# Adding three partial products into the same 256 PSUM columns, in the input and up-projections of a hybrid RWKV-7 / latent-attention layer

## The chip, the cores and the metric

The kernel runs on one core of a Trainium2 chip. The metric is device time in microseconds (us) of one execution, the median of several runs. TensorE (PE in the profile) does the matmuls and loads weights (PEld), VectorE is DVE, ScalarE is ACT, GpSimd is POOL, and SyncE (SP) issues most DMAs.

## The reference

One decoder layer over 256 tokens of width 2048, in float32:

```python
h = rms_norm(x, attn_norm_g[l])
proj = h @ w_in[l]
shifted = token_shift(proj[..., :RWKV_SHIFT_DIM], rwkv_mu[l])
h_r, h_k, h_v, h_w, h_a, h_g = _split(shifted, IN_SPLITS[:6])
c_q, c_kv, k_pe = _split(proj[..., RWKV_SHIFT_DIM:], IN_SPLITS[6:])
y_rwkv = rwkv7_mixer(h_r, h_k, h_v, h_w, h_a, h_g, ...)
y_mla = mla_mixer(c_q, c_kv, k_pe, positions, ...)
x = x + concatenate([y_rwkv, y_mla]) @ w_out[l]
h = rms_norm(x, ffn_norm_g[l])
x = x + conv_glu_ffn(h, ...)
return rms_norm(x, final_norm_g)
```

`rwkv7_mixer` is a recurrence over 16 heads of 64, with a group norm and a gate behind it. `mla_mixer` is causal attention with 8 heads; it normalises `c_q` and `c_kv` (512 wide each) and projects them up to queries (`w_uq`), keys and values. `conv_glu_ffn` is a gated MLP of width 5632. The input projection has 3360 + 1024 + 64 columns, the up-projections of queries and keys 20 tiles of 128 columns.

## The kernel before, in words

A float32 product is made from three products of shorter numbers. Weights and activations are each split into a high part (the value rounded to the type that PE reads fast, fp32r) and a low part (what is left). The kernel adds w_hi·x_hi + w_hi·x_lo + w_lo·x_hi.

Weights come in pieces of 128 x 1024 (`piece`, L125 to L137): SP loads `raw`, ACT casts it to `hi` (L133), DVE subtracts to get `lo` (L134; for the second piece of input tiles 17 to 24 POOL does). The high and low parts of the activations lie side by side, as 2 x 256 columns for each step of 128 rows.

`prod_b` multiplies one piece: for each step a 512-wide matmul of w_hi against [x_hi | x_lo] (L165), so that columns 0:256 of the PSUM tile hold w_hi·x_hi and columns 256:512 hold w_hi·x_lo; then for each step a 256-wide matmul of w_lo against x_hi, into columns 0:256 (L168). `joined` evicts the tile in three operations: ACT copies columns 256:512 (L173), DVE adds columns 0:256 (L174), DVE multiplies by a scale for each token (L175). The scale is that of the RMS norm: `rsB` for the input, `rrB` for the two latents.

`in_tile(i)` (L191) makes one of 35 output tiles of 128 columns of the input projection, from two pieces of 8 steps, 32 matmuls in all. `up_b` (L797) makes two up tiles of 4 steps each from one piece; there are 20 up tiles: 4 `qr` (rotary queries), 8 `qn` and 8 `kn`. The FFN uses `prod_b` and `joined` too (L961 to L972).

`shifted` (L371) evicts an input tile into `h` and mixes it with its neighbour token; that feeds the recurrence's preparation. Gram products of the prepared rows (`gram`, PE L527, evicted at L532 into `G`) go to DRAM by DMA (`dL`, L540) and back in another layout (`Lp`, L569). DVE scales `Lp` (L578) and solves triangular systems in 31 steps (L582, L584). While that runs, PE goes on with input tiles 18 and up. Then follow the latent tiles `cr`, the up-projections of the rotary queries and the values, the chunks of the recurrence (L677, with `px`, `pS`, `py` in PSUM and `XB`, `UV`, `ST` made by DVE), the other up-projections, the group norm (L719 to L741: `gmu`, `gva`, `gsq`, with a reciprocal square root `ry` on POOL), transposes `pyT` (L745) for the output product, the attention scores (`psc`, `mx`, `pexp`), the output projection and the FFN.

A PSUM tile comes from one of three rings: `mm` with 3 tiles, `ch` with 3, `at` with 2. Rings of SBUF hold 3 `raw`, 3 `hi`, 3 `lo` and 7 small tiles. The order of instructions in each engine's queue isn't that of the code: a scheduler that simulates the timeline sets it, by operands, rings and its own costs, on all engines (SP's only in the opening is written by hand). So a change of an eviction can move other instructions.

Of the kernel before, what the change touches and what calls it, by code (L numbers as in the profile page):

```python
# [14 lines left out]
ALU = mybir.AluOpType  # L15
AX = mybir.AxisListType

P = 128
T = 256
# [35 lines left out]
def hybrid_layer(ctx: ExitStack, tc: tile.TileContext, a: dict, out: bass.AP):  # L55
    nc = tc.nc
    V, S, PE = nc.vector, nc.scalar, nc.tensor
# [8 lines left out]
    def nm(s):  # L66
        uid[0] += 1
        return f"{s}{uid[0]}"
# [3 lines left out]
    def s4(dt=F32, n="s4"):  # L72
        return sb.tile([P, 1024], dt, tag="s4", name=nm(n), bufs=NS4)
# [11 lines left out]
    def t1(n, w=T, dt=F32):  # L85
        return sb.tile([P, 260], dt, tag="t1", name=nm(n), bufs=NT1)[:, :w]

    def t2(n, w=T, dt=F32):
        return sb.tile([P, 384], dt, tag="t2", name=nm(n), bufs=NT2)[:, :w]

    def st(n, w):
        return sb.tile([P, 32], F32, tag="st", name=nm(n), bufs=8)[:, :w]

    def mm(n="mm"):
        return ps.tile([P, 512], F32, tag="mm", name=nm(n), bufs=NMM)
# [4 lines left out]
    def at(n="at"):  # L100
        return ps.tile([P, 512], F32, tag="at", name=nm(n), bufs=NAT)

    def con(shape, n, dt=F32):
        return sb.tile(shape, dt, name=n, bufs=1)
# [10 lines left out]
    def vv(name, i, rows=slice(0, P)):  # L115
        return vec[rows, VOFF[name] + i:VOFF[name] + i + 1]
# [8 lines left out]
    def piece(src, dst=None, eng=None):  # L125
        raw = sb.tile([P, 1024], F32, tag="raw", name=nm("raw"), bufs=NRAW)
        last_w[0] = nc.sync.dma_start(raw, src).ins
        if dst is None:
            hi = sb.tile([P, 1024], F32R, tag="hi", name=nm("hi"), bufs=NHI)
            lo = sb.tile([P, 1024], F32R, tag="lo", name=nm("lo"), bufs=NLO)  # L130
        else:
            hi, lo = (dst.rearrange("p k t -> p (k t)")[:, q * 1024:(q + 1) * 1024] for q in range(2))
        S.copy(hi, raw)  # L133
        sub = (eng or V).tensor_tensor(lo, raw, hi.bitcast(F32), ALU.subtract).ins  # L134
        if eng is None:
            last_lo[0] = sub
        return hi, lo  # L137

    def xsplit(g):
        raw = s4(n="xraw").rearrange("p (k t) -> p k t", k=4)  # L140
        nc.sync.dma_start(raw, xT[:, g * 4:(g + 1) * 4, :])
        for j in range(4):
            k = g * 4 + j
            h = xs_[g][:, j, 0, :]
            S.activation(h, raw[:, j, :], AF.Copy, scale=vv("ag", k))
            last_x[0] = V.scalar_tensor_tensor(xs_[g][:, j, 1, :], raw[:, j, :], vv("ag", k),
                                               h.bitcast(F32), ALU.mult, ALU.subtract).ins
        return raw
# [5 lines left out]
    def flush(every=False):  # L154
        now = [f for n, f in pend if n == 0 or every]
        pend[:] = [(n - 1, f) for n, f in pend if n > 0 and not every]
        for f in now:
            f()
# [3 lines left out]
    def prod_b(acc, pieces, act, kt0, n, first, last):  # L162
        hi, lo = pieces
        for j in range(n):
            PE.matmul(acc, hi[:, j * P:(j + 1) * P], act(kt0 + j), start=first and j == 0, stop=False,  # L165
                      skip_group_check=True)
        for j in range(n):
            PE.matmul(acc[:, :T], lo[:, j * P:(j + 1) * P], act(kt0 + j)[:, 0, :], start=False,  # L168
                      stop=last and j == n - 1, skip_group_check=True)


    def joined(dst, acc, scale, rows=slice(0, P)):
        S.copy(dst, acc[rows, T:])  # L173
        V.tensor_tensor(dst, acc[rows, :T], dst, ALU.add)  # L174
        V.tensor_tensor(dst, dst, scale[rows], ALU.mult)  # L175


    def prod_a(accs, pieces, act_hi, act_lo, kt0, n, first, last, tbs=(0, 1)):
# [10 lines left out]
    x_hl = lambda k: xs_[k // 4][:, k % 4, :, :]  # L189

    def in_tile(i, pf=mm):  # L191
        acc = pf()
        for h in range(2):
            eng = nc.gpsimd if h and 17 <= i < 25 else None
            prod_b(acc, piece(a["win"][i, h], eng=eng), x_hl, h * 8, 8, h == 0, h == 1)
        flush()
        return acc

# [108 lines left out]
    acc0 = [mm(), mm(), at()]  # L307
    pcs = {}
# [4 lines left out]
    def sums(h):  # L313
        for tb in range(2):
            t, o = s4(n="xt"), h * 2 + tb
            nc.sync.dma_start(t, a["x"][tb * P:(tb + 1) * P, h * 1024:(h + 1) * 1024])
            S.activation(t, t, AF.Square, accum_out=ssx[:, o:o + 1])

    with tc.manual_schedule(engines={mybir.EngineType.SP}):
        for g in range(4):  # L320
            xsplit(g)
            if g == 0:
                nc.scalar.dma_start(cst, a["cst"])
            if g % 2 == 0:
                for i in range(2):
                    pcs[i, g // 2] = piece(a["win"][wt0[i], g // 2])
            for i in range(2):
                hl = tuple(u[:, (g % 2) * 512:(g % 2 + 1) * 512] for u in pcs[i, g // 2])
                prod_b(acc0[i], hl, x_hl, g * 4, 4, g == 0, g == 3)
        for h in range(2):  # L330
            prod_b(acc0[2], piece(a["win"][26, h]), x_hl, h * 8, 8, h == 0, h == 1)
        sums(0)
        kacc[0] = in_tile(1)
        dve0 = last_lo[0]
        sums(1)
        kacc[1] = in_tile(2, ch)
        rope_tables()
        lora = s4(n="lora")
        nc.sync.dma_start(lora, a["lora"])

    rsB = sb.tile([P, T], F32, tag="rsB", name="rsB", bufs=1)
# [30 lines left out]
    def shifted(acc, i, rows=slice(0, P), dst=None):  # L372
        h = t1("h", 257)
        nc.gpsimd.memset(h[rows, 0:1], 0.0)
        joined(h[rows, 1:257], acc, rsB, rows)
        o = t1("sh") if dst is None else dst
        S.activation(o[rows], h[rows, 1:257], AF.Copy, scale=om_mu[rows, i:i + 1])
        V.scalar_tensor_tensor(o[rows], h[rows, 0:256], vv("mu", i, rows), o[rows], ALU.mult, ALU.add)
        return o
# [49 lines left out]

    acc = acc0[2]  # L430
    kraw, ksw = t1("kraw"), t1("ksw")
    joined(kraw[0:64], acc, rsB, slice(0, 64))
    shifted(acc, 26, rows=slice(64, 96), dst=sg2)
    sigmoid_(sg2, slice(64, 96))
    nc.gpsimd.dma_start(kraw[64:128], kraw[0:64])
# [11 lines left out]
    for p in range(8):  # L447
        pp, g = p // 2, p % 2
# [3 lines left out]
        acc = kacc[p] if p in kacc else in_tile(1 + p)  # L452
# [45 lines left out]
    for p in range(8):  # L498
        pp, g = p // 2, p % 2
        acc = in_tile(9 + p)  # L500
# [254 lines left out]
    cl, rrs, rrB = [], [], []  # L755

    def latent(x, gname, post):
        c_ = [s4(F32R, "cl").rearrange("p (k s t) -> p k s t", k=2, s=2) for _ in range(2)]
        ssum = t2("css")
        for j in range(4):  # L760
            acc = in_tile(27 + x * 4 + j)
            cr = t2("cr")
            joined(cr, acc, rsB)
            if j == 0:
                S.activation(ssum, cr, AF.Square)
            else:
                sq = t2("csq")
                S.activation(sq, cr, AF.Square)
                V.tensor_tensor(ssum, ssum, sq, ALU.add)
            h_, l_ = (c_[j // 2][:, j % 2, q, :] for q in range(2))  # L770
            S.activation(h_, cr, AF.Copy, scale=vv(gname, j))
            V.scalar_tensor_tensor(l_, cr, vv(gname, j), h_.bitcast(F32), ALU.mult, ALU.subtract)
        pss = at("pss")
        for tb in range(2):
            PE.matmul(pss[:, tb * 2:tb * 2 + 2], ssum[:, tb * P:(tb + 1) * P], ones[:, 0:2], start=True, stop=True)
        m = st("ssm", 2)
        V.tensor_copy(m, pss[:, 0:4:2])
        rr = con([P, 2], f"rr{x}")
        V.tensor_scalar(rr, rsqrt(m, 1.0 / 512, EPS, 2), post, None, ALU.mult)
        rb = con([P, T], f"rrB{x}")  # L780
        bcast(rr, rb, at, t2)
        rrs.append(rr)
        rrB.append(rb)
        cl.append(c_)
# [12 lines left out]
    def up_b(src, i, x, dsts):  # L797
        pcs = piece(src[i])
        for j in range(2):
            acc = mm()  # L800
            prod_b(acc, (pcs[0][:, j * 512:(j + 1) * 512], pcs[1][:, j * 512:(j + 1) * 512]),
                   lambda k: cl[x][k // 2][:, k % 2, :, :], 0, 4, True, True)
            joined(dsts[j], acc, rrB[x])

    for i in range(4, 6):
        up_b(a["wuq"], i, 0, [qr[:, (i - 4) * 2 + j, :] for j in range(2)])
# [145 lines left out]
    for blk, nf in enumerate((24, 20)):  # L952
        hh = [s4(F32R, "hh").rearrange("p (k t) -> p k t", k=4) for _ in range(nf // 4)]
        hl = [s4(F32R, "hl").rearrange("p (k t) -> p k t", k=4) for _ in range(nf // 4)]
        for fi in range(nf):
            f = f0 + fi
            accs = []
            for gu in range(2):
                acc = mm()
# [24 lines left out]
        n = nf // 2  # L984
# [105 lines left out]
```

## Time and profile before

| | us |
|---|---|
| median of 3 runs | 1208.74 (1208.29 to 1209.25) |
| span of the profiled execution | 1203.6 |
| PE busy | 1159.9 (96% of the span) |
| DVE busy | 839.1 (70%) |
| ACT busy | 599.4 (50%) |
| POOL busy | 77.4 (6%) |

The profiled execution's own time is its span, 1203.6 us; what lies around the span makes up the rest of the 1208.74. Rows of the trace give the start and the length in us, engine, line of the kernel, operation, output and inputs by name, shape and how many instructions; in square brackets the engine's idle time before it and what ended that. Rows of groups give the smallest, median and largest duration in ns. The rows of the table by stage begin with the stretch and its length, then the busy time of each engine with the number of instructions, the granted clock of PE, the share of time in which DMA engines worked, and GB/s.

### The profile page before, as it was taken

How to read it: one execution, taken by the hardware profiler on the slowest of the kernel's cores; microseconds unless marked ns; L12 is line 12 of the kernel's file. 1: busy time of each engine (PE TensorE's matmuls, PEld its weight loads, DVE VectorE, ACT ScalarE, POOL GpSimd, SP SyncE). 2: the span in 40 equal slices, each digit the busy share in tenths (PEclk: the TensorE clock that was granted, in tenths of full speed). 3: DMA queues.
4: the chain of work that ended last, by engine and by line, in shares of the span. 5: the costliest groups of instructions: out<-in, count | busy, mean ns of one | idle time of the engine just before them, and what ended most of it. 6: DMA issues, size and time to landing. Idle time of an engine off the chain costs nothing.

```text
span 1203.6 us, 18439 instructions
## 1 busy us (share of the span) xinstructions
PE 1159.9 (96%) x6993; PEld 990.6 (82%) x6993; DVE 839.1 (70%) x1352; ACT 599.4 (50%) x939; POOL 77.4 (6%) x214
## 2 busy tenths in 40 slices
PE   7899998998799999999999999999999999999996
PEld 6788877887577888888888888888888888888885
DVE  6898749977887556777777776444577777775563
ACT  6784434633444455655555554333455555554442
POOL 1500042002110001000000000000000000000000
PEclk9899998999999999999999999999999999999999
DMA  8555443754133555655555555555655555566662
GB/s 317 177 155 159 138 143 122 213 168 147 62 140 114 184 172 175 206 190 191 187 192 191 191 192 191 193 190 190 200 191 192 192 193 193 192 223 202 205 217 81
DMA packets 71017, 215.82 MB, mean 179 GB/s; under 512 B 17616, under 2 KB 17872, under 8 KB 70928
## 3 DMA queue, kind: packets, MB, share of 16 engines
q1 hardware_dynamic: 69776, 211.84, 53.9%
q10 hardware_dynamic: 768, 2.05, 0.5%
q8 instruction: 55, 0.90, 0.3%
q0 software_dynamic: 384, 0.75, 0.2%
q14 instruction: 34, 0.28, 0.1%
HBM read 210.48 MB, written 3.41 MB: 178 GB/s over the span
## 4 chain that ended last, share of the span: by engine, by line
PE 84%; DVE 8%; DMA 3%; POOL 2%; issue 1%; ACT 1%; SPq 1%; ACTq 0%; DVEq 0%; POOLq 0%
PE mm L165 34%; PE mm L168 17%; PE mm L185 9%; PE mm L187 9%; PE mm L186 9%; DVE lo L134 2%; PE pg L527 1%; DMA xt<-in_x 1%; PE px L677 1%; DMA Lp<-dL 1%; DMA raw<-in_win 0%; POOL cosR L291 0%; DMA dT<-Tq 0%; PE py L677 0%; SPq L540 0%
## 5 line engine op out<-in xcount | busy, mean ns | idle before, releaser
L134 DVE TENSOR_TENSOR lo<-raw,hi 128x1024 fp32r<-128x1024 f32 x368 | 453.0, 1231 | 288.0 <-ACT hi L133 283.1
L133 ACT CAST hi<-raw 128x1024 fp32r<-128x1024 f32 x376 | 395.5, 1052 | 451.7 <-issue 234.9
L165 PE MATMUL mm<-z,hi 128*128 128x512 f32 x1408 | 351.3, 392 | 0.0
L165 PEld LDWEIGHTS mm<-z,hi 128*128 128x128 f32 x1408 | 251.9, 188 | 43.7
L168 PEld LDWEIGHTS mm<-z,lo 128*128 128x128 f32 x1408 | 188.3, 188 | 14.5
L168 PE MATMUL mm<-z,lo 128*128 128x256 f32 x1408 | 191.6, 278 | 0.0
L165 PE MATMUL mm<-x,hi 128*128 128x512 f32 x528 | 144.4, 410 | 17.9 <-DVE h L174 9.6
L186 PE MATMUL mm<-lo,hh 128*128 128x512 f32 x336 | 130.7, 389 | 0.0
L187 PE MATMUL mm<-hi,hl 128*128 128x512 f32 x336 | 130.7, 389 | 0.0
L165 PEld LDWEIGHTS mm<-x,hi 128*128 128x128 f32 x528 | 97.0, 195 | 35.6 <-ACT hi L133 8.3
L185 PE MATMUL mm<-hi,hh 128*128 128x512 f32 x336 | 119.7, 389 | 0.0
L168 PEld LDWEIGHTS mm<-x,lo 128*128 128x128 f32 x528 | 74.7, 193 | 7.4 <-issue 1.0
L168 PE MATMUL mm<-x,lo 128*128 128x256 f32 x528 | 79.9, 288 | 0.0
L186 PEld LDWEIGHTS mm<-lo,hh 128*128 128x128 f32 x336 | 63.1, 188 | 13.1
L187 PEld LDWEIGHTS mm<-hi,hl 128*128 128x128 f32 x336 | 63.1, 188 | 13.1
L185 PEld LDWEIGHTS mm<-hi,hh 128*128 128x128 f32 x336 | 63.1, 188 | 13.0
L186 PE MATMUL mm<-lo,yhi 128*128 128x512 f32 x128 | 51.1, 399 | 0.0
L187 PE MATMUL mm<-hi,ylo 128*128 128x512 f32 x128 | 50.5, 394 | 0.0
L185 PE MATMUL mm<-hi,yhi 128*128 128x512 f32 x128 | 49.6, 405 | 0.0
L964 POOL MEMSET gt<- 128x2 f32 x44 | 4.3, 100 | 575.8 <-DVE hl L976 558.9
L187 PEld LDWEIGHTS mm<-hi,ylo 128*128 128x128 f32 x128 | 24.1, 188 | 5.6 <-DVE ylo L749 0.4
L185 PEld LDWEIGHTS mm<-hi,yhi 128*128 128x128 f32 x128 | 23.9, 188 | 5.7 <-DVE kn L174 0.8
(291 smaller groups left out, 1142.8 us busy)
## 6 DMA issues: line engine op xcount, KB each, us to landing
raw<-in_wgu SPq DMA_DIRECT2D x176, 512.0 KB, 3.3
raw<-in_wdn SPq DMA_DIRECT2D x88, 512.0 KB, 4.1
raw<-in_win SPq DMA_DIRECT2D x70, 512.0 KB, 3.7
raw<-in_wout SPq DMA_DIRECT2D x32, 512.0 KB, 3.4
raw<-in_wuq SPq DMA_DIRECT2D x6, 512.0 KB, 3.3
xraw<-in_xT SPq DMA_DIRECT2D x4, 512.0 KB, 6.3
xt<-in_x SPq DMA_DIRECT2D x4, 512.0 KB, 6.7
raw<-in_wuv SPq DMA_DIRECT2D x4, 512.0 KB, 3.3
```

What stands on the lines that cost most here:

```text
L133: S.copy(hi, raw)
L134: sub = (eng or V).tensor_tensor(lo, raw, hi.bitcast(F32), ALU.subtract).ins
L165: PE.matmul(acc, hi[:, j * P:(j + 1) * P], act(kt0 + j), start=first and j == 0, stop=False, skip_group_check=True)
L168: PE.matmul(acc[:, :T], lo[:, j * P:(j + 1) * P], act(kt0 + j)[:, 0, :], start=False, stop=last and j == n - 1, skip_group_check=True)
L185: PE.matmul(accs[tb], ah, wh, start=first and j == 0, stop=False)
L186: PE.matmul(accs[tb], ah, wl, start=False, stop=False)
L187: PE.matmul(accs[tb], al, wh, start=False, stop=last and j == n - 1)
L527: PE.matmul(pg[h][:, o:o + P], BK[pp][hs, gg, w * 2 + r, :, :], AR[pp][hs, gg, w * 2 + r, :, :], start=o == 0, stop=True, skip_group_check ...
L677: PE.matmul(dst[HS[h], a_ * 64:(a_ + 1) * 64], lhsT, rhs, start=n == 0 and a_ == 0, stop=True, skip_group_check=True)
L964: nc.gpsimd.memset(gt[:, 0:2], 0.0)
```

## The change

A new product `prod_c` splits each 512-wide matmul in two of 256, w_hi·x_hi and w_hi·x_lo, and adds both, and the w_lo·x_hi product, into columns 0:256. Columns 256:512 stay unused. A new eviction `scaled` is one DVE operation: columns 0:256 times the scale. The input tiles (`in_tile` and the three of the opening) and the up tiles use the two; the FFN keeps `prod_b` and `joined`. Lines of the new kernel behind the new functions lie 12 further down.

```diff
--- before.py
+++ after.py
@@ -168,11 +168,23 @@
             PE.matmul(acc[:, :T], lo[:, j * P:(j + 1) * P], act(kt0 + j)[:, 0, :], start=False,
                       stop=last and j == n - 1, skip_group_check=True)
 
-
-    def joined(dst, acc, scale, rows=slice(0, P)):
-        S.copy(dst, acc[rows, T:])
-        V.tensor_tensor(dst, acc[rows, :T], dst, ALU.add)
-        V.tensor_tensor(dst, dst, scale[rows], ALU.mult)
+    def prod_c(acc, pieces, act, kt0, n, first, last):
+        hi, lo = pieces
+        for j in range(n):
+            for s in range(2):
+                PE.matmul(acc[:, :T], hi[:, j * P:(j + 1) * P], act(kt0 + j)[:, s, :],
+                          start=first and j == 0 and s == 0, stop=False)
+        for j in range(n):
+            PE.matmul(acc[:, :T], lo[:, j * P:(j + 1) * P], act(kt0 + j)[:, 0, :], start=False,
+                      stop=last and j == n - 1)
+
+    def joined(dst, acc, scale):
+        S.copy(dst, acc[:, T:])
+        V.tensor_tensor(dst, acc[:, :T], dst, ALU.add)
+        V.tensor_tensor(dst, dst, scale, ALU.mult)
+
+    def scaled(dst, acc, scale, rows=slice(0, P)):
+        V.tensor_tensor(dst, acc[rows, :T], scale[rows], ALU.mult)
 
 
     def prod_a(accs, pieces, act_hi, act_lo, kt0, n, first, last, tbs=(0, 1)):
@@ -192,7 +204,7 @@
         acc = pf()
         for h in range(2):
             eng = nc.gpsimd if h and 17 <= i < 25 else None
-            prod_b(acc, piece(a["win"][i, h], eng=eng), x_hl, h * 8, 8, h == 0, h == 1)
+            prod_c(acc, piece(a["win"][i, h], eng=eng), x_hl, h * 8, 8, h == 0, h == 1)
         flush()
         return acc
 
@@ -326,9 +338,9 @@
                     pcs[i, g // 2] = piece(a["win"][wt0[i], g // 2])
             for i in range(2):
                 hl = tuple(u[:, (g % 2) * 512:(g % 2 + 1) * 512] for u in pcs[i, g // 2])
-                prod_b(acc0[i], hl, x_hl, g * 4, 4, g == 0, g == 3)
+                prod_c(acc0[i], hl, x_hl, g * 4, 4, g == 0, g == 3)
         for h in range(2):
-            prod_b(acc0[2], piece(a["win"][26, h]), x_hl, h * 8, 8, h == 0, h == 1)
+            prod_c(acc0[2], piece(a["win"][26, h]), x_hl, h * 8, 8, h == 0, h == 1)
         sums(0)
         kacc[0] = in_tile(1)
         dve0 = last_lo[0]
@@ -372,7 +384,7 @@
     def shifted(acc, i, rows=slice(0, P), dst=None):
         h = t1("h", 257)
         nc.gpsimd.memset(h[rows, 0:1], 0.0)
-        joined(h[rows, 1:257], acc, rsB, rows)
+        scaled(h[rows, 1:257], acc, rsB, rows)
         o = t1("sh") if dst is None else dst
         S.activation(o[rows], h[rows, 1:257], AF.Copy, scale=om_mu[rows, i:i + 1])
         V.scalar_tensor_tensor(o[rows], h[rows, 0:256], vv("mu", i, rows), o[rows], ALU.mult, ALU.add)
@@ -429,7 +441,7 @@
 
     acc = acc0[2]
     kraw, ksw = t1("kraw"), t1("ksw")
-    joined(kraw[0:64], acc, rsB, slice(0, 64))
+    scaled(kraw[0:64], acc, rsB, slice(0, 64))
     shifted(acc, 26, rows=slice(64, 96), dst=sg2)
     sigmoid_(sg2, slice(64, 96))
     nc.gpsimd.dma_start(kraw[64:128], kraw[0:64])
@@ -760,7 +772,7 @@
         for j in range(4):
             acc = in_tile(27 + x * 4 + j)
             cr = t2("cr")
-            joined(cr, acc, rsB)
+            scaled(cr, acc, rsB)
             if j == 0:
                 S.activation(ssum, cr, AF.Square)
             else:
@@ -798,9 +810,9 @@
         pcs = piece(src[i])
         for j in range(2):
             acc = mm()
-            prod_b(acc, (pcs[0][:, j * 512:(j + 1) * 512], pcs[1][:, j * 512:(j + 1) * 512]),
+            prod_c(acc, (pcs[0][:, j * 512:(j + 1) * 512], pcs[1][:, j * 512:(j + 1) * 512]),
                    lambda k: cl[x][k // 2][:, k % 2, :, :], 0, 4, True, True)
-            joined(dsts[j], acc, rrB[x])
+            scaled(dsts[j], acc, rrB[x])
 
     for i in range(4, 6):
         up_b(a["wuq"], i, 0, [qr[:, (i - 4) * 2 + j, :] for j in range(2)])
```

## The prediction

> **What bounds the kernel now.** I read the sums by stage first: busy time of PE, PEld (its weight loads), DVE, ACT and POOL, the granted PE clock, DMA share and GB/s.
>
> ```profile
> 60.00:177.00 117.00, 116.55 (x739) 100.32 (x739) 91.88 (x186) 61.59 (x105) 17.32 (x26) 1.00 0.47 142
> 177.00:188.00 11.00, 4.99 (x19) 4.02 (x18) 6.95 (x20) 2.95 (x7) 0.82 (x4) 0.70 0.56 211
> 188.00:242.00 54.00, 52.44 (x311) 45.73 (x309) 51.20 (x98) 32.00 (x55) 7.77 (x7) 1.00 0.59 171
> 242.00:288.00 46.00, 45.53 (x673) 39.55 (x672) 35.40 (x70) 19.88 (x35) 8.83 (x32) 1.00 0.49 150
> 288.00:326.00 38.00, 26.31 (x465) 22.48 (x464) 29.58 (x45) 11.92 (x23) 5.13 (x14) 0.96 0.23 82
> 326.00:369.00 43.00, 40.82 (x203) 30.20 (x201) 37.56 (x76) 18.83 (x44) 6.14 (x14) 1.00 0.38 133
> 480.00:1203.00 723.00, 713.91 (x3813) 615.77 (x3811) 473.77 (x658) 352.84 (x499) 4.11 (x41) 1.00 0.58 191
> ```
>
> From 480 us on, PE works 713.91 of 723 us: that is the FFN, which the change leaves alone. What can be gained lies before. There PE waits at 177 to 188 (4.99 of 11 us busy) and from 288 to 326 (26.31 of 38); DVE is at 95% (51.20 of 54) in 188:242, yet PE at 97% too, so not much is lost there. The second view is the chain that ended last, in the FFN, where the same product runs undisturbed (start, length, what), and the sum of L165 over a long piece of it.
>
> ```profile
> 482.94 1.83 PE mm L165 x8
> 484.77 0.91 PE mm L168 x8
> 485.68 1.83 PE mm L165 x8
> 487.51 0.94 PE mm L168 x8
> ```
>
> ```profile
> 482.93:731.03 248.10, 179.44 (x721) 128.71 (x721) 1.00 0.57 192
> ```
>
> Eight 512-wide matmuls take 1.83 us (229 ns each), eight 256-wide ones 0.91 to 0.94. The 721 matmuls in 248.10 us are 90 such groups, so a whole group of 8 + 8 takes 248.10/90 = 2.757 us, and 2.757 − 1.83 = 0.927 is 8 × 116 ns. The third view is the chain around the wait at 177.8, and the engines' own rows there.
>
> ```profile
> 166.18 1.98 PE pg L527 x24
> ...
> 174.15 1.55 DMA dL<-G
> ...
> 175.82 6.07 DMA Lp<-dL
> ...
> 181.92 1.24 DVE Lp L578
> ...
> 183.66 0.34 DVE h L174
> ...
> 184.05 3.78 PE mm L165 x8
> ```
>
> ```profile
> 176.98 1.07 PE L168 MATMUL mm<-x,lo 128*128 128x256 f32 x8
> 184.05 3.78 PE L165 MATMUL mm<-x,hi 128*128 128x512 f32 x8 [6.01 <-DVE h L174]
> 187.63 1.37 PE L168 MATMUL mm<-x,lo 128*128 128x256 f32 x8
> ```
>
> ```profile
> 179.60 1.23 DVE L134 TENSOR_TENSOR lo<-raw,hi 128x1024 fp32r<-128x1024 f32 x1 [6.43 <-ACT hi L133]
> ```
>
> The last Gram product ends at 168.16. Its result goes to DRAM (dL) and back (Lp, 6.07 us), and DVE scales it at 181.92. In DVE's queue the eviction of input tile 18 stands behind that scaling, so tile 21, which needs that PSUM buffer, waits 6.01 us. The clock then falls: its first 8 matmuls take 3.78 us instead of 1.83, the next 1.37 instead of 1.07. The stall costs 6.0 + 1.95 + 0.3 = 8.3 us.
>
> **The change part by part.**
>
> *Split of the 512-wide matmul.* 35 input tiles with 16 and 20 up tiles with 4 make 640 hi matmuls; each becomes two of 256. Eight pairs take 16 × 0.116 = 1.853 us against 1.83, that is +0.023, and 80 such groups give **+1.9 us**. With 0.91 or 0.94 per eight it is −0.8 to +4. The added weight loads are the point to check. Their rows in the FFN (min, median, max in ns) are these:
>
> ```profile
> L168 PEld LDWEIGHTS mm<-z,lo x1408: 187/188/188, 469.2 to 1084.6; 128*128 128x128 f32 x176
> ```
>
> A load lasts 188 ns, yet the 256-wide matmuls, each with a load of its own, follow each other every 116 ns and add into the same columns: the loads overlap, and same-column accumulation costs nothing extra. PE waits for neither.
>
> The Trainium skill speaks against this ("TensorE: Matmul & The Clock Gate", Part 3, The mechanism: a weight load overlaps running matmuls only if its row group differs). By that rule the sum would be the last rival's below; this trace's 116 ns disagrees.
>
> *Evictions.* What goes are the copy L173 (ACT), the sum L174 and one of two DVE operations; one stays. The sums up to 470 us of L173, L174 and L175:
>
> ```profile
> 0.00:470.00 470.00, 20.28 (x56) 0.98 0.51 162
> ```
> ```profile
> 0.00:470.00 470.00, 23.31 (x56) 0.98 0.51 162
> ```
> ```profile
> 0.00:470.00 470.00, 23.29 (x56) 0.98 0.51 162
> ```
>
> With 55 or 56 evictions by 0.37 and 0.42 us, 20 us of ACT and 23 us of DVE go. Where PE is over 97% busy they are hidden, so they are counted by stage only.
>
> *177 us.* PE, around the last Gram (pg); mm_1921 is input tile 19, before:
>
> ```order
> L165 MATMUL mm_1921<-x_66,hi_1924 128x512 x4
> L168 MATMUL mm_1921<-x_65,lo_1925 128x256 x4
> L527 MATMUL pg_1709<-AR_498,BK_502 128x128 x4
> L527 MATMUL pg_1722<-AR_498,BK_502 128x128 x2
> L527 MATMUL pg_1723<-AR_498,BK_502 128x128 x2
> ```
>
> and after, where mm_2054 is input tile 18:
>
> ```order
> L178 MATMUL mm_2054<-x_65,lo_2058 128x256
> L539 MATMUL pg_2002<-AR_574,BK_578 128x128 x4
> L178 MATMUL mm_2054<-x_65,lo_2058 128x256 x2
> L539 MATMUL pg_2003<-AR_574,BK_578 128x128 x4
> L559 MATMUL pt_2032<-cst,BK_578 128x128 x2
> L178 MATMUL mm_2054<-x_65,lo_2058 128x256
> L178 MATMUL mm_2054<-x_66,lo_2058 128x256 x4
> ```
>
> So the last Gram moves one input tile ahead. DVE at the eviction of tile 18 (h_1904 before, h_2198 after), first before:
>
> ```order
> L134 TENSOR_TENSOR lo_2040<-raw_2037,hi_2039 128x1024
> L134 TENSOR_TENSOR lo_2093<-raw_2090,hi_2092 128x1024
> L578 TENSOR_TENSOR Lp_1766<-Lp_1766,Mp 128x1024
> L582 TENSOR_TENSOR tm_1822<-Tq_1821,Lp_1766 128x31
> L584 TENSOR_TENSOR Tq_1821<-Tq_1821,tm_1822 128x31
> L174 TENSOR_TENSOR h_1904<-mm_1776,h_1904 128x256
> ```
>
> and after:
>
> ```order
> L134 TENSOR_TENSOR lo_2284<-raw_2281,hi_2283 128x1024
> L590 TENSOR_TENSOR Lp_2046<-Lp_2046,Mp 128x1024
> L134 TENSOR_TENSOR lo_2360<-raw_2357,hi_2359 128x1024
> L594 TENSOR_TENSOR tm_2116<-Tq_2115,Lp_2046 128x31
> L187 TENSOR_TENSOR h_2198<-mm_2054,rsB 128x256
> L596 TENSOR_TENSOR Tq_2115<-Tq_2115,tm_2116 128x31
> L187 TENSOR_TENSOR h_2274<-mm_2213,rsB 128x256
> ```
>
> The eviction still stands behind the Lp scaling, now with a lo behind it, and all DVE work queued there waits for the load Lp. Before, from the Gram's end to the scaling went 181.92 − 168.16 = 13.76 us; scaling, lo, one small operation and the eviction add 1.24 + 1.23 + 0.2 + 0.42, so tile 21 can start some 16.8 us behind the Gram. PE has meanwhile the rest of tile 18 (about 4.3 us of Gram, transposes and lo products) and two tiles of 5.5 us (2 × 2.757): 15.3 us, against 177.8 − 168.2 = 9.7 before. A wait of 1.5 us is left of 6.0, too short, I think, to bring the clock down. −4.5 − 1.95 − 0.3 = −6.8; I take **−6**, since SP's queue has other transfers there. Bounds: −8.3 (all of it) and 0 (the Gram's inputs come no earlier on DVE, and PE waits for them instead).
>
> *Start, and 60:242.* At 42 us PE waits for an eviction:
>
> ```profile
> 42.59 3.75 PE L165 MATMUL mm<-x,hi 128*128 128x512 f32 x8 [3.20 <-DVE h L174]
> ```
> ```profile
> 40.55 0.42 DVE L229 COPY rsB<-rsb 128x256 f32<-128x256 f32 x1
> ```
>
> The sum at 42.02 did not need the norm scale rsB; the new single operation does. But rsB is copied at 40.55, ahead of it in the same queue before and after: nothing lost, nothing won here, −0.5 for the later 8 us (bounds −3 to 0). In 188:242 PE is idle 1.56 us (54 − 52.44): −0.5 (0 to −1.6).
>
> *288 to 369.* The reachable waits are these, on PE:
>
> ```profile
> 321.59 0.74 PE L168 MATMUL mm<-cl,lo 128*128 128x256 f32 x4 [2.13 <-DVE lo L134]
> ...
> 323.18 1.02 PE L677 MATMUL py<-UV,G 128*64 128x64 f32 x15 [0.85 <-DVE UV L694]
> ```
> ```profile
> 369.13 1.17 PE L745 MATMUL pyT<-cst,yt 128*128 128x128 f32 x8 [1.97 <-DVE yt L741]
> ```
>
> The recurrence's own waits on XB and UV hold no eviction, since the q evictions begin only at 324.6:
>
> ```profile
> L174 DVE TENSOR_TENSOR qn<-mm,qn x8: 406/418/425, 324.6 to 352.4; 128x256 f32<-128x256 f32 x8
> ```
>
> After the change the scores' maxima (mx) and the second group norm (gmu) come behind the last up-projection on DVE, before:
>
> ```order
> L849 TENSOR_REDUCE mx_3805<-psc_3803 128x1
> L719 TENSOR_REDUCE gmu_3846<-yt_2408 128x16
> L174 TENSOR_TENSOR kn_3346<-mm_3666,kn_3346 128x256
> ```
>
> and after:
>
> ```order
> L187 TENSOR_TENSOR kn_3834<-mm_4264,rrB_3822 128x256
> L134 TENSOR_TENSOR lo_4552<-raw_4549,hi_4551 128x1024
> L861 TENSOR_REDUCE mx_4333<-psc_4331 128x1
> L861 TENSOR_REDUCE mx_4349<-psc_4347 128x1
> L861 TENSOR_REDUCE mx_4333<-psc_4331 128x1
> L731 TENSOR_REDUCE gmu_4374<-yt_2784 128x16
> ```
>
> DVE's chain from gmu to the transposes pyT ran from here to 369.13:
>
> ```profile
> 344.39 1.21 DVE L719 TENSOR_REDUCE gmu<-yt 128x16 f32<-128x1024 f32 x1
> ...
> 361.33 1.23 DVE L727 TENSOR_TENSOR yt<-yt,ry 128x1024 f32<-128x1024 f32 x1 [1.94 <-POOL ry L219]
> ```
>
> 24.7 us, 5.7 of it evictions and lo that are gone from it; what stands ahead of gmu adds 2.7: 21.7 us from the last up-projection. PE has meanwhile 18 output products, the rest of two score sets, four gates and four score sets, from these rows about 18.5 us (4.1 for four gate matmuls, 1.73 per score set):
>
> ```profile
> 355.07 1.02 PE L739 MATMUL pgate<-g2a,sg 128*128 128x512 f32 x2
> ...
> 359.18 0.50 PE L185 MATMUL mm<-hi,yhi 128*128 128x512 f32 x1
> ...
> 363.81 0.32 PE L838 MATMUL psc<-cmb,idb 128*128 128x384 bf16 x1 [0.26 <-ACT pexp L850]
> ...
> 365.54 0.32 PE L838 MATMUL psc<-cmb,idb 128*128 128x384 bf16 x1
> ```
>
> The pyT wait becomes 3.2 instead of 1.97, +1.2 (up to +4.2 if no DVE work leaves the chain). Ahead of it the waits of 2.13 and 0.85 go, because the up tiles fill in: −3. Net **−2**; bounds −6.4 (these waits, the pyT wait and shorter DVE turns) and +4.2.
>
> Sum: +1.9 − 6 − 0.5 − 0.5 − 2 = −7.1. The span was 1203.6, the median of the runs 1208.74, 5.1 more for what lies around it; I leave that as it is. 1208.7 − 7.1 = **1201.6 us**.
>
> **The rivals.**
>
> *No change.* The freed time was hidden, and Lp comes as late as before because the Gram's inputs are made by the same DVE chain (91.88 of 117 us busy in 60:177, so there is slack that hides evictions). Only the split is left: 1208.7 + 1.9 = 1210.6, or 1208 with small gains. Against it: the Gram stands earlier in PE's queue, and some 20 evictions before it have each lost one of 0.42, 8 us of DVE work.
>
> *Slower.* The group norm's chain, moved behind the last up-projection, decides: pyT waits 6.2 instead of 1.97 (+4.2), with +1.9 for the split, and the gain at 177 fails: 1214.8. It turns the sign as soon as 177 gives back less than about 6 us. For it: DVE is the late one at 369. Against: with the evictions gone, DVE reaches gmu earlier.
>
> *Bare weight loads.* If each added load of 188 ns were exposed, 640 × 0.188 = 120 us: 1329. The steady 116 ns rows are against it. This is the rule on row groups in the Trainium skill ("TensorE: Matmul & The Clock Gate", Part 3, The mechanism) taken as it is written.
>
> **How the numbers follow.** Forecast 0.65, no change 0.14, slower rival 0.18, bare loads 0.03. The measurement can tell about 0.2%, 2.4 us. The forecast's own ends, all at once, are −20.1 and +8.2; they won't all meet. I go from 1190, where the wait at 177 and most of the waits after 288 are gone, to 1213, which holds no change and half of the slower case. Left out: bare loads, the worst of the slower case, some of the best. Chances: faster 0.65, same 0.14, slower 0.21.
>
> **What would show it.** In the profile after: eight hi pairs on the chain of input tiles in 1.83 to 1.88 us; up to 470 us no row of the copy or the sum (L173, L174 before) and one DVE row of 0.42 us per eviction; PE's wait before tile 21 at 1 to 3 us and a clock of 1.00 there; the wait before pyT at 3 us. Wrong: pairs of eight over 2 us, a wait on pg's inputs (AR, BK) of 4 us or more ahead of the Gram, a wait of 6 us at tile 21, or one over 5 us at pyT. The FFN should take as long as before.

## The result, and the profile after

| | before | changed |
|---|---|---|
| median of 6 runs each, us | 1209.14 (1208.29 to 1212.53) | 1200.43 (1196.53 to 1201.20) |
| ratio to before, 95% interval | | 0.992 (0.9896 to 0.9944) |
| span of the profiled execution, us | 1203.6 | 1198.3 |
| PE busy / idle in the span, us | 1159.9 / 43.7 | 1164.2 / 34.1 |
| DVE, ACT busy, us | 839.1, 599.4 | 817.5, 582.9 |

The kernel is faster by 0.8%, 8.7 us between the medians. The two profiled executions differ by 5.3 us only: that of before was one of its faster ones (its span with the 1.7 us that lay around the changed kernel's, 1200.04 against 1198.3, makes 1205.3). In every run on record whose span is known, 1.7 to 1.9 us lie around the span; so most of the 5.1 us that were put down to it ahead of the result (1208.74 − 1203.6) is the difference between runs. What follows splits the 5.3 us: PE idles 9.6 us less and works 4.3 us more.

The table by stage of the changed kernel (stretch, its length, busy time of PE, PEld, DVE, ACT, POOL, granted PE clock, DMA share, GB/s):

```profile
60.00:177.00 117.00, 117.00 (x999) 113.81 (x998) 81.24 (x167) 56.66 (x87) 16.96 (x28) 1.00 0.49 150
177.00:188.00 11.00, 8.51 (x72) 8.25 (x71) 10.66 (x23) 6.69 (x13) 3.67 (x4) 1.00 0.41 137
188.00:242.00 54.00, 50.94 (x569) 50.29 (x567) 47.19 (x85) 24.31 (x36) 6.88 (x9) 0.97 0.66 196
288.00:326.00 38.00, 36.08 (x454) 29.00 (x453) 32.45 (x47) 15.13 (x24) 5.97 (x14) 1.00 0.42 140
326.00:369.00 43.00, 38.77 (x230) 32.71 (x230) 34.19 (x62) 16.72 (x35) 5.03 (x14) 0.92 0.30 99
480.00:1198.00 718.00, 708.38 (x3778) 610.74 (x3776) 469.64 (x652) 349.40 (x496) 4.08 (x41) 1.00 0.58 191
```

The wait at 177 is smaller, 2.5 us of 11 instead of 6.0, but 188:242 is worse (3.1 us idle instead of 1.6). The large step is at 288:326, 36.08 us busy instead of 26.31. That stretch is the recurrence, and its PE time between the first and last product of `px` and `py` (L677) shows it best; before first, then after:

```profile
251.60:325.10 73.50, 61.40 (x861) 0.98 0.30 104
```
```profile
245.80:321.10 75.30, 73.38 (x992) 0.97 0.37 122
```

PE idled 12.1 us in the recurrence before, and idles 1.9 us there now. The recurrence itself got no shorter (75.3 us instead of 73.5): more other products lie in its waits, 48.3 us of PE time instead of 35.9 (the busy time above less that of L677, L689 in the changed kernel). These are its longest waits for XB, UV and ST before, and below them the only two that are left:

```profile
295.64 0.69 PE L677 MATMUL px<-XB,TT 128*64 128x64 f32 x16 [2.69 <-DVE XB L688]
297.56 0.37 PE L677 MATMUL pS<-UV,BKt 128*64 128x64 f32 x1 [1.23 <-DVE UV L694]
308.32 0.69 PE L677 MATMUL py<-ST,AR 128*64 128x64 f32 x16 [1.87 <-DVE ST L707]
```
```profile
298.86 0.69 PE L689 MATMUL px<-XB,TT 128*64 128x64 f32 x16 [1.40 <-DVE XB L700]
300.07 0.33 PE L689 MATMUL pS<-UV,BKt 128*64 128x64 f32 x2 [0.52 <-DVE UV L706]
```

The recurrence begins 5.8 us earlier, and the FFN's first product follows at 462.0 instead of 467.6:

```profile
L165 PE MATMUL mm<-z,hi x1408: 388/392/483, 462.0 to 1078.1; 128*128 128x512 f32 x176
```

The chain at the solve. The critical chain of the changed kernel, and PE's own rows behind it:

```profile
158.10 1.10 PE pg L539 x8
...
165.56 1.54 DMA dL<-G
...
167.12 6.14 DMA Lp<-dL
...
173.29 0.06 DVE Lp L590
```
```profile
167.82 2.05 PE L175 MATMUL mm<-x,hi 128*128 128x256 f32 x16
169.70 1.10 PE L178 MATMUL mm<-x,lo 128*128 128x256 f32 x8
170.65 2.04 PE L175 MATMUL mm<-x,hi 128*128 128x256 f32 x16
...
179.92 0.44 PE L627 MATMUL pv<-cst,sh 128*128 128x128 f32 x2 [2.49 <-DVE sh L390]
...
194.56 0.41 PE L627 MATMUL pv<-cst,sh 128*128 128x128 f32 x2 [2.97 <-DVE sh L390]
```

The load Lp is scaled at 173.3, 8.6 us earlier than before (181.92). No input tile waits for a PSUM buffer there any more. Instead the transposes of the values (`pv`) wait 2.49 and 2.97 us for `sh`, which DVE makes from the evicted tile between the steps of the solve. The first three rows also show the split's price: from 167.82 to 170.65 one group of 24 matmuls takes 2.83 us, where the FFN's 8 + 8 take 2.757. Near the end the wait before the transposes `pyT` grew, as the prediction's term for 288 to 369 had it, to 4.23 us from 1.97:

```profile
361.74 1.94 PE L757 MATMUL pyT<-cst,yt 128*128 128x128 f32 x8 [4.23 <-DVE yt L753]
```

### The profile page after: what moved, and what is told of

Read it like the earlier page. It is cut to its first block, busy times and chain, and to the rows that moved or that the text cites. A ratio compares the mean times of both kernels' runs of the same rounds, so it can differ in the third digit from the quotient of the medians.

```text
span 1198.3 us, 19598 instructions
## 1 busy us (share of the span) xinstructions
PE 1164.2 (97%) x7633; PEld 1026.2 (86%) x7633; DVE 817.5 (68%) x1296; ACT 582.9 (49%) x883; POOL 77.3 (6%) x214
## 4 chain that ended last, share of the span: by engine, by line
PE 91%; DVE 4%; DMA 2%; issue 1%; ACT 1%; SPq 1%; POOL 0%; ACTq 0%; POOLq 0%
PE mm L165 27%; PE mm L168 14%; PE mm L175 10%; PE mm L197 9%; PE mm L198 9%; PE mm L199 9%; PE mm L178 5%; PE pg L539 1%; PE px L689 1%; DVE Tq L596 1%; DMA xraw<-in_xT 1%; PE py L689 1%; DMA Lp<-dL 1%; DVE lo L134 0%; DMA xt<-in_x 0%
## 5 line engine op out<-in xcount | busy, mean ns | idle before, releaser
L165 PEld LDWEIGHTS mm<-z,hi 128*128 128x128 f32 x1408 | 251.9, 188 | 43.7
L175 PE MATMUL mm<-x,hi 128*128 128x256 f32 x1056 | 149.6, 289 | 11.6 <-ACT hi L133 8.2
L175 PEld LDWEIGHTS mm<-x,hi 128*128 128x128 f32 x1056 | 135.7, 194 | 14.5 <-ACT hi L133 8.2
L178 PE MATMUL mm<-x,lo 128*128 128x256 f32 x528 | 77.2, 285 | 0.0
L199 PEld LDWEIGHTS mm<-hi,hl 128*128 128x128 f32 x336 | 63.1, 188 | 13.1
L197 PEld LDWEIGHTS mm<-hi,hh 128*128 128x128 f32 x336 | 63.1, 188 | 13.1
L178 PEld LDWEIGHTS mm<-x,lo 128*128 128x128 f32 x528 | 69.4, 193 | 0.1
L198 PEld LDWEIGHTS mm<-lo,yhi 128*128 128x128 f32 x128 | 24.4, 190 | 5.0
```

The source lines that it names most:

```text
L175: PE.matmul(acc[:, :T], hi[:, j * P:(j + 1) * P], act(kt0 + j)[:, s, :], start=first and j == 0 and s == 0, stop=False)
L197: PE.matmul(accs[tb], ah, wh, start=first and j == 0, stop=False)
L198: PE.matmul(accs[tb], ah, wl, start=False, stop=False)
L199: PE.matmul(accs[tb], al, wh, start=False, stop=last and j == n - 1)
```

## The experiments

Twelve kernels ran, each beside the kernel before on the same chip. Times are medians; ratios are to the kernel before, with 95% intervals. The kernel before took 1209.1 to 1211.7 us in these rounds, so kernels of different rounds are compared by their ratios. "Recurrence idle" is the length of the stretch from first to last product of the recurrence less PE's busy time in it; "other work" is that busy time less the recurrence's own products, as the trace shows it (the expectations give it as it stands in PE's queue before the run, by the scheduler's costs); "last Gram" is the start of the last Gram product.

| kernel | us | ratio | recurrence idle | other work | last Gram |
|---|---|---|---|---|---|
| before | 1209.1 | 1 | 12.1 | 35.9 | 167.9 |
| changed | 1200.4 | 0.992 (0.9896 to 0.9944) | 1.9 | 48.3 | 160.4 |
| split_only | 1207.7 | 0.9989 (0.9969 to 1.001) | 5.0 | 43.3 | 164.4 |
| evict_only | 1206.6 | 0.9983 (0.9966 to 0.9999) | 12.3 | 33.6 | 159.3 |
| input_only | 1199.3 | 0.9916 (0.9893 to 0.994) | 3.4 | 50.9 | 160.0 |
| up_only | 1212.0 | 1.0021 (1.0003 to 1.0038) | 11.5 | 38.3 | 166.7 |
| before_gram_early | 1217.0 | 1.0069 (1.0042 to 1.0096) | 9.5 | 52.8 | 168.1 |
| gram_late | 1212.2 | 1.002 (1.0001 to 1.004) | 12.9 | 35.0 | 165.5 |
| evict_gram_early | 1201.2 | 0.993 (0.9906 to 0.9955) | 4.1 | 55.3 | 159.2 |
| ffn_split | 1211.4 | 1.0031 (1.0011 to 1.0052) | 1.9 | 48.0 | 161.1 |
| dve_back | 1216.2 | 1.0041 (1.0023 to 1.006) | 13.1 | 35.7 | 162.7 |
| act_back | 1200.4 | 0.9907 (0.9887 to 0.9927) | 1.9 | 48.0 | 161.4 |
| input_vlate | 1196.4 | 0.9875 (0.9857 to 0.9893) | 1.1 | 68.1 | 160.5 |
| input_vlate_dve_lo | 1195.2 | 0.9888 (0.986 to 0.9916) | 5.5 | 56.9 | 160.3 |

### The parts apart

**split_only**: before, with each hi matmul cut in two but each half in its own columns.

```diff
+            for s in range(2):
+                PE.matmul(acc[:, s * T:(s + 1) * T], hi[:, j * P:(j + 1) * P], act(kt0 + j)[:, s, :],
+                          start=first and j == 0 and s == 0, stop=False, skip_group_check=True)
```

> The kernel before, with each hi matmul of the input and up tiles cut in two of 256, but each half still in its own 256 columns and the old eviction of three operations. Theory (the split costs PE time, the saved evictions give the gain): in the trace after, a group of 24 matmuls of an input tile takes 24 x 118 ns = 2.83 us, before 2.757 to 2.785; 80 groups make +3.4 to +5.6, so 1212.5 to 1215. Rival 1 (the cost of the split is 1.9 us, as predicted): 1211. Rival 2 (not the evictions but the new order that any such edit brings gives the gain): faster than before, near 1200 to 1204.

It came out 0.1% below before, within the measurement, which none of the three expectations had. It saves no operation, and yet other products fill 7.1 of the 12.1 us of recurrence idle: the new order of the queues gave back what the split cost. So the recurrence's waits can be filled without a saved operation.

**evict_only**: the one-operation eviction behind the old 512-wide matmuls; it leaves out w_hi·x_lo in the input and up tiles.

```diff
-            prod_c(acc, piece(a["win"][i, h], eng=eng), x_hl, h * 8, 8, h == 0, h == 1)
+            prod_b(acc, piece(a["win"][i, h], eng=eng), x_hl, h * 8, 8, h == 0, h == 1)
```

> The changed kernel with its one-operation eviction, but with the 512-wide hi matmuls of before; columns 256:512 are written and never read, so the product w_hi x x_lo is left out of the input and up tiles. Theory (the saved operations give the gain, the split takes 3.4 to 5.6 us of it back): 1195 to 1197. Rival 1 (split costs 1.9): 1198.5. Rival 2 (the order alone): anything, 1200 to 1209, with no tie to the split's price.

This fell outside the theory: 1206.6, in the range of the second rival, the order alone. It has less work than the changed kernel on PE and the same on DVE and ACT, and yet is slower by half a per cent. Its last Gram starts at 159.3, before the changed kernel's, and still:

```profile
247.20:321.00 73.80, 61.52 (x843) 0.91 0.32 97
```

12.3 us idle in the recurrence, as before. The early part came forward; PE then ran out of other products in the recurrence (33.6 us of other work, 48.3 in the changed kernel). The theory that the saved operations are the gain had to be mended: they count through what they let be laid where.

**input_only** and **up_only**: the change in one kind of tile, the other as before.

> The change in the input tiles alone; up tiles keep the 512-wide matmul and three operations. Theory (most of the gain comes at the wait of 6 us at 177 us, whose evictions are those of input tiles; the 288 to 369 stage gives 2 of 7): 1202 to 1204. Rival (the up tiles' 16 evictions among the scores and the group norm give the most): 1205 to 1209.

> The change in the up tiles alone (20 tiles, 80 of the 640 hi matmuls). Theory (they give 2 of the 7 us): 1206 to 1208. Rival (they give most of it): 1201 to 1204. Rival 2 (pyT later on DVE, no gain there): 1209 to 1213.

The input tiles give all of it (0.9916; 1199.3 us is below the 1202 to 1204 expected), the up tiles alone make it 0.2% slower: the second rival on up_only is right, with a wait of 4.1 us before pyT, and 2 us for the later stage as a gain of the up tiles is not borne out.

### Where the gain comes from

The second theory: the freed time brings the last Gram products forward, so solve and recurrence begin while more input and up tiles are still to be done, and these fill the recurrence's waits.

**before_gram_early**: no operation changed; the Gram products are written ahead of tile 17.

```diff
+    flush()
     UV = [s4(n="UV").rearrange("p (e t) -> p e t", e=8) for _ in range(4)]
```

> The kernel before with no operation changed; only the last Gram products, their DMAs and the start of the solve are written ahead of input tile 17 instead of behind it, so that the scheduler lays them earlier. Theory now (what counts is how much other PE work is laid into the waits of the solve and the recurrence; the saved evictions matter only through that): in its queue 40 us of other PE work stand between the first and the last product of the recurrence, 29 in the kernel before, 38 in the changed one; so 1198 to 1202. Rival (the freed ACT and DVE time itself is the gain): the operations are those of before, 1207 to 1210.

The expectation failed: 0.7% slower. The last Gram still starts at 168.1: the scheduler left it where it was in PE's queue, and an input tile now waits 9.64 us for the eviction that stands behind the scaling of Lp:

```profile
182.00 3.78 PE L165 MATMUL mm<-x,hi 128*128 128x512 f32 x8 [9.64 <-DVE h L174]
```

An earlier place in the code gives nothing where the queue doesn't follow it. The inputs were not what held the Gram back. DVE writes the last of them, AR, within 0.3 us of the same time in this kernel, in the kernel before and in the changed one (in this order), and the changed one has its last Gram 7.5 us earlier than before:

```profile
150.38 0.43 DVE L505 TENSOR_TENSOR AR<-sh,AR 128x256 f32<-128x256 f32 x1
150.21 0.43 DVE L505 TENSOR_TENSOR AR<-sh,AR 128x256 f32<-128x256 f32 x1
150.11 0.43 DVE L517 TENSOR_TENSOR AR<-sh,AR 128x256 f32<-128x256 f32 x1
```

So what brought the last Gram forward in the changed kernel is its place in PE's queue. If the second theory means that freed DVE time had the inputs ready sooner, it isn't borne out; whether the scheduler's own timeline moved the Gram because of that time isn't on record.

**gram_late**: the changed kernel, with the Gram products, their DMAs and the solve one tile later.

```diff
-            pend.append((0, gram))
+            pend.append((p // 7, gram))
-    pend.append((0, solve_load))
-    pend.append((1, solve))
+    pend.append((1, solve_load))
+    pend.append((2, solve))
```

> The changed kernel with the last Gram products, their DMAs and the solve written one input tile later; all else as changed. Theory now: 25 us of other PE work are left between the first and last product of the recurrence (38 in the changed kernel), and the freed operations don't help: 1208 to 1214. Rival (the freed ACT and DVE time is the gain): 1200 to 1204.

As the theory had it: 1212.2, and the recurrence idles again, with 35.0 us of other work. So the freed operations alone don't help either.

```profile
252.80:328.90 76.10, 63.17 (x886) 0.88 0.31 96
```

**evict_gram_early**: evict_only with the line of before_gram_early.

> evict_only (one-operation eviction, 512-wide hi matmuls, w_hi x x_lo left out) with the Gram products written ahead of tile 17. Theory now: 44 us of other PE work in the recurrence, 26 in evict_only; so evict_only's 1206.6 falls by 10 or more, to 1192 to 1197, below the changed kernel by the price of the split. Rival (evict_only was slow for a cause of its own, its eviction or matmul): 1203 to 1207.

It falls from 1206.6 to 1201.2 as recurrence idle goes from 12.3 to 4.1. The direction is that of the theory, the size is half, between the two ranges expected.

**dve_back** and **act_back**: the changed kernel with one operation of the old size put back behind each eviction, in place: a maximum on DVE (in one), a copy on ACT (in the other).

```diff
     def scaled(dst, acc, scale, rows=slice(0, P)):
         V.tensor_tensor(dst, acc[rows, :T], scale[rows], ALU.mult)
+        V.tensor_tensor(dst, dst, dst, ALU.max)
```

```diff
+        S.copy(dst, dst)
```

> The changed kernel with one DVE operation of the old size put back behind each eviction (the maximum of the tile with itself, in place, 0.42 us, 56 times); only the ACT copy stays saved. Theory (DVE's freed 23 us bring the Gram's inputs forward, and with them the solve and the work laid into the recurrence; its queue now has 27 us of other PE work there, 38 in the changed one): 1208 to 1213, the gain gone. Rival (ACT's 20 us, the copy that came first in each eviction, are what counted): 1199 to 1203.

> The changed kernel with one ACT copy of the old size put back behind each eviction, in place (0.37 us, 56 times); only the DVE operation stays saved. Theory (DVE's time counts): 38 us of other PE work in the recurrence as in the changed kernel, 1199 to 1203. Rival (ACT's time counts): 1206 to 1211.

The two engines come out apart. With DVE's operation back the gain is gone (1.0041), with ACT's copy back it is all there (0.9907). The solve's 31 products (first and last start behind the durations), in the changed kernel and in dve_back:

```profile
L594 DVE TENSOR_TENSOR tm<-Tq,Lp x31: 184/357/427, 175.6 to 222.2; 128x31 f32<-128x31 f32 x2, 128x60 f32<-128x60 f32 x2, 128x87 f32<-128x87 f32 x2, 128x112 f32<-128x112 f32 x2
```
```profile
L595 DVE TENSOR_TENSOR tm<-Tq,Lp x31: 192/374/2443, 176.7 to 230.1; 128x31 f32<-128x31 f32 x2, 128x60 f32<-128x60 f32 x2, 128x87 f32<-128x87 f32 x2, 128x112 f32<-128x112 f32 x2
```

It begins 1.1 us later and ends 7.9 us later. The evictions stand between its steps, and ten of the added maxima lie there, 6.4 us of DVE's time (one took 2.63 us beside a subtraction on POOL):

```profile
176.70:230.40 53.70, 6.38 (x10) 0.97 0.51 158
```

That doesn't settle it, though: in the kernel before, with as many DVE operations for each tile, these products start 48.0 us apart from first to last, in dve_back 53.4. The recurrence, dve_back and act_back in turn:

```profile
252.60:329.10 76.50, 63.39 (x909) 0.94 0.34 106
```
```profile
244.90:319.90 75.00, 73.08 (x993) 0.97 0.38 123
```

Both edits also pass through the scheduler, and by its queues dve_back had only 27 us of other work to lay there, act_back 38. How much of dve_back's loss is DVE's time and how much the order isn't separated: its last Gram, at 162.7, is earlier than that of split_only (164.4), which has the same DVE operations and idles 5.0 us instead of 13.1.

### What the split costs

**ffn_split**: the changed kernel, with split and one-operation eviction in the FFN too.

```diff
-                    prod_b(acc, piece(a["wgu"][f, gu, h]), z_hl, h * 8, 8, h == 0, h == 1)
+                    prod_c(acc, piece(a["wgu"][f, gu, h]), z_hl, h * 8, 8, h == 0, h == 1)
-            joined(gt[:, 2:258], accs[0], rs2B)
+            scaled(gt[:, 2:258], accs[0], rs2B)
-            joined(up, accs[1], rs2B)
+            scaled(up, accs[1], rs2B)
```

> The changed kernel with the same split and one-operation eviction in the FFN too: 1408 more hi matmuls cut in two, in 176 groups of 8, where PE is busy 98 to 99% of the time. It prices the split alone. Prediction's price (0.023 us per group): +4.0, 1204.5. Price read in the trace after (24 x 117.8 ns = 2.827 us per group, 2.757 before): +12.3, 1212.7. If the saved evictions gave time here too, less than +4.

11.0 us more than the changed kernel by the medians (spans: 10.9), 13.4 by the ratios. Where PE sets the pace the saved evictions give nothing. From the first to the last of these products PE takes 628.4 us, where the changed kernel took 616.1 (462.0 to 1078.1):

```profile
L175 PE MATMUL mm<-z,hi x2816: 278/279/367, 460.3 to 1088.7; 128*128 128x256 f32 x188
```

That is 12.3 us for 176 groups, 0.070 us each, as expected from the trace. PE's rows there:

```profile
600.19 2.04 PE L175 MATMUL mm<-z,hi 128*128 128x256 f32 x16
602.07 1.10 PE L178 MATMUL mm<-z,lo 128*128 128x256 f32 x8
603.02 2.05 PE L175 MATMUL mm<-z,hi 128*128 128x256 f32 x16
```

A group takes 603.02 − 600.19 = 2.83 us. For the change's 80 groups 0.070 makes 5.6 us.

### A faster version

**input_vlate**: input_only with the four value projections written behind the query and key up-projections (the loop over `wuv` moved down).

> input_only (the change in the input tiles alone) with the value projections written behind the query and key up-projections instead of ahead of them, so that more up tiles lie in the recurrence: 54 us of other PE work between its first and last product, 39 in input_only. Theory (work laid there is hidden in waits): 1190 to 1196. Rival (the waits there are already filled; more only lengthens the recurrence): 1197 to 1203.

```profile
245.00:338.50 93.50, 92.36 (x1067) 0.97 0.41 129
```

1196.4 us, 0.9875 of before, just above the theory's range and below the rival's. The recurrence is stretched to 93.5 us, but PE works all but 1.1 of it. It beats before clearly; against the changed kernel its interval (0.9857 to 0.9893) lies just below that of the change (0.9896 to 0.9944), but the two did not run in one round, and act_back, which did run beside it, has 0.9887 to 0.9927.

**input_vlate_dve_lo**: the same, with the low parts of tiles 17 to 24 made by DVE.

```diff
-            eng = nc.gpsimd if h and 17 <= i < 25 else None
+            eng = None
```

> input_vlate with the low parts of tiles 17 to 24 made by DVE (1.22 us each, 8 of them) instead of POOL, where each takes 2.4 us and a DVE operation that starts beside it ends with it (2.2 to 2.6 us for one of 0.2 to 0.4). Theory (DVE's turn is what PE waits for at 177 and 191, 2.5 and 3.1 us; so 8 x (about 2.1 lost - 1.2) = 7 us less for DVE in the solve, and these waits shrink): 1192 to 1195. Rival (DVE's own queue grows by 9.8 us there, its queue lays only 45 us of other PE work in the recurrence where input_vlate has 54): 1197 to 1204.

In input_vlate POOL and DVE worked like this (POOL's row, then DVE's):

```profile
175.67 2.39 POOL L134 TENSOR_TENSOR lo<-raw,hi 128x1024 fp32r<-128x1024 f32 x1 [4.84 <-PE mm L175]
```
```profile
175.90 2.22 DVE L596 TENSOR_TENSOR Tq<-Tq,tm 128x31 f32<-128x31 f32 x1
175.56 0.42 DVE L187 TENSOR_TENSOR h<-mm,rsB 128x256 f32<-128x256 f32 x1
```

A solve step on 31 columns, 0.2 us elsewhere, takes 2.22 us and ends as POOL's subtraction ends. The Trainium skill ("SBUF — State Buffer", Terms) says why: the two engines take a shared port pair in turns, held for a whole instruction; the rows agree, 178.12 us for the end of the step and 178.06 for that of the subtraction. With POOL's share gone PE no longer waits at `pv`, from 170 to 200 us (input_vlate, then this kernel):

```profile
170.00:200.00 30.00, 24.72 (x208) 24.29 (x208) 26.20 (x46) 13.82 (x22) 9.87 (x11) 1.00 0.49 157
```
```profile
170.00:200.00 30.00, 30.00 (x257) 29.99 (x256) 26.66 (x56) 17.82 (x29) 0.39 (x4) 1.00 0.62 195
```

Yet the whole run is 1195.2, a ratio of 0.9888 against 0.9875: no difference that can be told. Of PE's 5.3 us won at 170 to 200, 4.4 came back as idle time in the recurrence (5.5 us instead of 1.1; 56.9 us of other work instead of 68.1). The local theory held, its number for the whole missed its range by 0.2 us.

## Why the prediction was right, and where it wasn't

The total was right: −7.1 us forecast (0.59%), 0.56 to 1.04% measured. Of its steps some held and some failed, and their errors cancelled; that the sum came out so near is partly luck.

**The Gram one tile earlier: held.** The last Gram starts at 160.4 instead of 167.9 and Lp is scaled 8.6 us earlier. It came from the order in PE's queue, as the prediction read it there, and not from inputs made sooner: the last of them is written at 150.6 us before and 150.5 now, some ten us ahead of the Gram. split_only, which saves no operation, has the Gram at 164.4. At tile 21 there is no wait for the buffer at all, where 1.5 us was forecast.

**−6 at 177: the place was wrong.** The step said that PE's wait for the tile's PSUM buffer shrinks and nothing takes its place. The buffer's wait went, but the transposes `pv` now wait for `sh`, 2.49 and 2.97 us. Over 170 to 200 us PE is busy 24.54 us where it was 23.99, half a microsecond more, with a clock of 0.94 instead of 0.89 (the changed kernel, then before):

```profile
170.00:200.00 30.00, 24.54 (x194) 24.11 (x194) 26.06 (x47) 13.09 (x21) 9.29 (x11) 0.94 0.47 157
```
```profile
170.00:200.00 30.00, 23.99 (x132) 20.59 (x132) 19.90 (x40) 14.61 (x28) 10.01 (x12) 0.89 0.40 128
```

What takes the place of the old wait is DVE in the solve, held up beside POOL. In the changed kernel each of the two waits at `pv` ends right behind such a step (POOL's row, then DVE's, at the second; the first follows a step of 2.17 us at 176.00):

```profile
191.28 2.46 POOL L134 TENSOR_TENSOR lo<-raw,hi 128x1024 fp32r<-128x1024 f32 x1 [4.23 <-ACT hi L133]
```
```profile
191.46 2.55 DVE L596 TENSOR_TENSOR Tq<-Tq,tm 128x240 f32<-128x240 f32 x1
193.94 0.47 DVE L390 SCALAR_TENSOR_TENSOR sh<-h,vec,sh 128x256 f32<-128x256 f32 x1
```

The neighbouring steps on 231 and 247 columns take 0.39 and 0.42 us. With POOL's share moved these waits are gone (input_vlate_dve_lo). The trace of before has such steps too, so they could have been read there, one of 2.55 us behind one of 0.33:

```profile
188.82 0.33 DVE L582 TENSOR_TENSOR tm<-Tq,Lp 128x175 f32<-128x175 f32 x1
189.19 2.55 DVE L584 TENSOR_TENSOR Tq<-Tq,tm 128x175 f32<-128x175 f32 x1
```

The −0.5 for 188 to 242 failed with it: PE idles 3.1 us there instead of 1.6, and the second wait at `pv` is 2.97 of them.

**−2 from 288 to 369: the step that failed.** The prediction let the up tiles fill two waits there, of 2.13 and 0.85 us, and these did go. The recurrence's own waits, on XB and UV (and ST), it set aside because no eviction lies in them. They needed none: products of other tiles fill these too, if they are still to be done when the recurrence begins. Of the 10.2 us of idle time that went, about 7 were given no term, as much as the whole forecast. gram_late and dve_back put the idle time back (12.9 and 13.1 us). The other half of the step, the later group norm, held: pyT waits 4.23 us, +2.3, between the +1.2 taken and the +4.2 allowed.

**+1.9 for the split: mis-sized.** It is 5.6 by ffn_split (0.070 per group instead of 0.023), over the upper bound of 4. The error was to price narrow matmuls by the 8 that follow wide ones, at 116 ns. In an unbroken run 24 of them take 2.83 us, 118 ns each, against 2.757 for the old group.

**Nothing for the removed ACT copies: held.** act_back costs nothing.

**Nothing at 42 us, −0.5 for the rest of the start.** The wait is still there, 3.39 us instead of 3.20, and from 8 to 60 us PE idles 3.6 us instead of 3.5, so the half microsecond didn't come:

```profile
42.04 3.65 PE L175 MATMUL mm<-x,hi 128*128 128x256 f32 x16 [3.39 <-DVE h L187]
```

The rivals: the group norm's chain did become later, but the gain outweighed it, so the slower case did not come; up_only shows it at work, 0.2% slower. Bare weight loads did not come: from 60 to 177 us the loads were busy 113.81 us of 117 and PE did not idle. "No change" would have been right for evict_only, whose Gram was as early: that it wasn't so for the changed kernel hung on the order the scheduler laid out, which the prediction read at the Gram but not in the recurrence.

Still open: how the order comes about, and how much of any single ratio is its accident. Where the gain lies is shown: other work fills the recurrence's waits, and recurrence idle mostly falls as that work grows, from 12 to 13 us at 34 to 36 us of it to 1.1 at 68. That the saved DVE operations are what put the work there is argued only. dve_back and act_back speak for it; split_only, which saves none and fills 7.1 us, and evict_only, which saves them all and fills nothing, speak for the order that the scheduler happens to lay. No run holds the order fixed and changes the operations alone. Recurrence idle doesn't rank all kernels either: before_gram_early idles 9.5 us there and is the slowest, since it lost 9.6 us ahead of it.

## What to carry to other kernels

What an edit of the evictions is worth depends on where other work lands in the queues: here the gain showed in a long serial stage that waits, far from the operations that were saved, and an edit that saved none won most of that idle time too. Before crediting a removed wait, name the next instruction in the queue and the engine it needs. Price a changed instruction in an unbroken run of its own kind, not by a row that follows another kind.

## What the runs showed of the hardware

- Weight loads of 188 ns, one for each matmul, overlap so far that 256-wide matmuls follow each other every 118 ns; PEld is then busy 113.81 of 117 us. Adding two products into the same columns costs nothing more: split_only adds into separate columns, and its group takes the same 2.83 us (172.12 to 174.95).
- A DVE solve step of 0.2 to 0.4 us that starts beside a POOL subtraction of 2.4 us lasts until that ends, to within 0.3 us. With 8 such subtractions moved to DVE, where each takes 1.2 us, PE was busy 5.3 us more of the 30 from 170 to 200 us; the queues' order differed too.
